# A transformer block with sixteen experts on one core: expert weights in 2 MB blocks with paired rows, and a gathering for two experts at once

## The chip, the core and the metric

The kernel runs on one core of a Trainium2 chip. Five engines work side by side: TensorE (PE, with its weight loads shown apart as PEld), VectorE (DVE), ScalarE (ACT), GpSimd (POOL) and SyncE (SP). Each has its own instruction queue; semaphores order them. In this kernel every transfer between the memory (HBM) and the on-chip buffers is issued by SP and carried by the core's 16 DMA engines. PE reads its operands from the on-chip buffers and writes its sums to the accumulation memory (the tiles `pa`, `pb`, `pd` and `pe`).

The metric is the device time of one execution in microseconds, the median of several runs. MiB below is 1,048,576 bytes; the diff's "2 MB" blocks are 2 MiB.

## The reference, cut to what matters

One layer: normalisation, a joint projection into four kinds of token mixers, an output projection with a gated residual, and then, as the last and longest stage, an expert layer in which every one of 16 experts chooses 64 of the 512 tokens:

```python
def expert_choice_ffn(h, w_router, w_gate, w_up, w_down):
    B, N, D = h.shape
    cap = EC_FACTOR * N // N_EXPERTS
    aff = jax.nn.softmax((h @ w_router).astype(F32), axis=-1)
    gate, idx = lax.top_k(jnp.swapaxes(aff, 1, 2), cap)
    xg = jax.vmap(lambda hb, ib: hb[ib])(h, idx)
    hid = jax.nn.silu(jnp.einsum('becd,edf->becf', xg, w_gate)) * jnp.einsum('becd,edf->becf', xg, w_up)
    y = jnp.einsum('becf,efd->becd', hid, w_down) * gate[..., None].astype(h.dtype)
    return jax.vmap(lambda yb, ib: jnp.zeros((N, D), yb.dtype).at[ib.reshape(-1)].add(yb.reshape(-1, D)))(y, idx)
...
        x_lat = x_lat + m_lat[5] * expert_choice_ffn(h_lat, w_router[l], w_gate[l], w_up[l], w_down[l])
...
    return rmsnorm(x_lat, final_norm_g)
```

Tokens are 1,024 wide, the hidden width of an expert is 2,048, and all is 32-bit floating point. An expert's three weight matrices are 8 MiB each, so an expert reads 24 MiB and the stage 384 MiB, every byte once.

## The kernel before

The program is straight-line code: Python loops unroll into one instruction list for each engine, and a scheduler sets the order on every engine when the program is built. Nearly all compute instructions are recorded in one helper, line 58 (L58), so the trace is read by the names of tiles.

**Routing.** While the output projection still runs, the residual `XL` (four tiles of 128 tokens) is transposed on PE for the router. DVE then finds each expert's 64 tokens in eight rounds of a maximum and a replacement (`RT`); a matmul with a triangular matrix turns the marks into `slot`, which says for each token and expert which of the 64 places it takes. `xn2` holds the normalised tokens, `a2` and `mcol` the scale and shift of each column.

**One expert.** DVE compares `iota` with `slot` to a one-hot matrix `OH` (in tile `OX`). Gathering: 8 matmuls with `OH` as the stationary operand (64 columns) and 512 columns of `xn2` moving, half of the width in each column half of the array; ACT copies the sum to `xgn`, PE transposes it in 8 pieces and DVE applies scale and shift, which gives `xg`, the 64 tokens by columns. Gate and up: 128 rows of a weight matrix at a time (`k` from 0 to 7) are the moving operand, and `xg` is the stationary one; 64 tokens fill half of the array's columns, so two halves of the hidden width are summed in the two column halves (`pgt` and `pup`, both tiles `pb`). ACT and DVE make `hid`, PE transposes it in 8 pieces to `hT`, and 16 row blocks of the down matrix are summed in `pa`. DVE multiplies by the gate of the layer (`m5`) into `y`. `weighted()` multiplies the one-hot matrix by the routing weights `aff` and transposes it (`OT`), and in the next expert four `add` steps multiply `OT` with `y` and add the product into `XL`, one token tile each.

A 32-bit matmul stands in the trace as two records, a transpose as one.

**The weight ring.** `wchunk` takes the next buffer of a ring of 18 of 1 MiB each (128 partitions of 2,048 numbers) and issues one DMA on SP's queue. A gate or up block is 128 weight rows, one row of 8 KB to a partition. A down block is 256 rows; a partition gets two rows of 4 KB that lie apart. The ring's buffers come in three pools, since the space comes free at three times: `ringa` (8) after the mixers, `ringm` (4) during the output projection, `ringb` (6) after it. Expert 0's last gate and up blocks go to four half-size `spare` buffers. Each DMA also waits for the DMA eight places ahead of it on the queue, because eight semaphores are used in turn; so at most eight are under way. SP issues in program order, and a buffer's next DMA waits for the matmuls that read it.

**The end.** The last expert's down product is taken in three blocks of columns (384, 384 and 256), so that the additions, the squares for the final norm (ACT) and the product with `gfin` (POOL) of one block run beside the next one's matmuls; rows of these transfers are 1,536 and 1,024 bytes.

## Time and profile before

| | |
|---|---|
| median of 3 runs | 1511.62 us (1509.63 to 1512.53) |
| the profiled execution's own time | 1509.62 us |
| its span, first to last instruction | 1507.8 us |
| PE busy | 1378.6 us, 91% |
| DVE busy | 458.1 us, 30% |
| ACT busy | 314.1 us, 21% |
| POOL busy | 237.8 us, 16% |
| moved by DMA | 481.57 MB, 319 GB/s over the span |
| granted PE clock, mean | 0.980 |

The page gives busy times, a strip of 40 slices of the span with the granted clock and the DMA rate, the chain of work that ended last, and the costliest groups. The trace behind it answers narrower questions: each engine's timeline, what an engine's queue waited for, busy times and DMA rate in chosen stretches. A busy share is a mean over stages with different limits: the first third of this span has idle DMA engines, the rest has not. The granted clock is a share of full speed: 1.00 is 2.4 GHz, 0.50 is 1.2 GHz.

### The profile page before, as it was taken

Reading aid. Unit: us, or ns where it says so; the run is one execution under the profiler, and the core shown is the slowest. Engines: PE = TensorE matmul, PEld = TensorE weight load, DVE = VectorE, ACT = ScalarE, POOL = GpSimd, SP = SyncE. Lnnn points to the kernel's source line nnn. Section 1 sums busy time; section 2 is a strip of 40 time slices with the busy share of each in tenths; the row PEclk is TensorE's granted clock in tenths of the full one; section 3 lists DMA queues with packets and bytes.
Section 4 is the critical chain, followed back from the end, with each engine's and each line's share of the span. In section 5 each row is a group of like instructions: output and inputs, shape, how many; then the busy total and the mean of one; then the engine's idle time right before and its main releaser. Section 6 shows DMA issues by size and latency. Waiting matters only on the chain.

```text
span 1507.8 us, 20244 instructions
## 1 busy us (share of the span) xinstructions
PE 1378.6 (91%) x8278; PEld 673.1 (45%) x8278; DVE 458.1 (30%) x998; ACT 314.1 (21%) x658; POOL 237.8 (16%) x229
## 2 busy tenths in 40 slices
PE   5998979989889979999999999999999999999996
PEld 3665767767557823333233233332332332333334
DVE  4657732444573640111211211211202112112012
ACT  5424316624573300011010010010010100100103
POOL 2425637431265100000000000000000000000002
PEclk9999989999999979999999999999999999999998
DMA  9341450646883769999999999999999999999995
GB/s 357 116 136 53 119 123 17 178 145 157 259 270 100 323 254 412 414 418 415 414 421 413 416 417 414 418 415 414 420 414 417 418 413 419 415 414 419 414 404 199
DMA packets 128270, 481.57 MB, mean 319 GB/s; under 512 B 34225, under 2 KB 43057, under 8 KB 94514
## 3 DMA queue, kind: packets, MB, share of 16 engines
q1 hardware_dynamic: 128178, 480.29, 82.1%
q8 instruction: 65, 1.06, 0.3%
q14 instruction: 27, 0.22, 0.0%
HBM read 468.84 MB, written 11.40 MB: 318 GB/s over the span
## 4 chain that ended last, share of the span: by engine, by line
PE 75%; DVE 9%; issue 5%; ACT 4%; DMA 3%; POOL 1%; SPq 1%; ACTq 0%; DVEq 0%; POOLq 0%
PE pb L58 33%; PE pa L58 31%; PE pd L58 7%; PE pe L58 5%; DMA wm<-in_wmod 1%; ACT A L58 1%; DVE RT L58 1%; DVE hid L58 1%; DVE tmpb L58 1%; DVE OY L58 1%; ACT hT L58 1%; DMA co<-in_cosq 1%; DVE acc L58 1%; SPq L1054 1%; DVE TB L58 1%
## 5 line engine op out<-in xcount | busy, mean ns | idle before, releaser
L58 PE MATMUL pb<-w,OX 128*64 128x512 f32 x2032 | 453.6, 598 | 0.9 <-DVE OX L58 0.9
L58 PE MATMUL pa<-w,hT 128*64 128x512 f32 (+2 forms) x1152 | 278.9, 549 | 0.1
L58 PEld LDWEIGHTS pb<-w,OX 128*64 128x64 f32 x2032 | 139.9, 137 | 305.2 <-issue 285.9
L1709 POOL TENSOR_TENSOR xo<-XL,gfin 128x384 f32<-128x384 f32 (+1 forms) x12 | 10.6, 913 | 955.9 <-DVE XL L58 955.9
L58 ACT ACTIVATE hid<-pb 128x512 f32<-128x512 f32 x32 | 17.4, 594 | 595.6 <-PE pb L58 595.6
L58 PEld LDWEIGHTS pa<-w,hT 128*64 128x64 f32 x1152 | 89.9, 136 | 114.2 <-issue 108.1
L58 DVE TENSOR_TENSOR hid<-hid,pb 128x512 f32<-128x512 f32 x32 | 20.6, 685 | 276.7 <-PE pb L58 276.7
L58 PE MATMUL pa<-xn,OX 128*64 128x512 f32 x256 | 102.2, 600 | 0.8 <-DVE OX L58 0.8
L58 PE MATMUL pa<-hh,wh 128*128 128x512 f32 (+1 forms) x240 | 89.7, 387 | 7.2 <-DVE dff L58 4.3
L58 PE MATMUL pa<-hh,wl 128*128 128x512 f32 (+1 forms) x240 | 86.2, 372 | 1.3 <-POOL wl L250 1.3
L58 PE MATMUL pd<-OY 64*128 64x512 f32 x120 | 67.3, 641 | 10.3 <-DVE OY L58 10.3
L58 DVE TENSOR_TENSOR XL<-XL,pd 128x512 f32<-128x512 f32 x60 | 41.2, 686 | 100.5 <-PE pe L58 76.5
L58 PE MATMUL pe<-OY 64*128 64x512 f32 x120 | 67.3, 641 | 0.0
L250 POOL TENSOR_TENSOR wl<-wr,wh 128x1024 fp32r<-128x1024 f32 (+1 forms) x22 | 50.7, 2305 | 75.5 <-ACT wh L58 72.9
L58 ACT ACTIVATE xgn<-pa 64x512 f32<-64x512 f32 x32 | 18.9, 592 | 208.7 <-PE pa L58 208.5
L58 DVE TENSOR_TENSOR OX<-OX,aff 128x256 f32<-128x256 f32 x16 | 6.8, 426 | 169.7 <-PE pa L58 169.7
L58 PEld LDWEIGHTS pa<-hh,wh 128*128 128x128 f32 x240 | 47.1, 197 | 23.7 <-issue 5.3
L58 DVE TENSOR_TENSOR XL<-XL,pe 128x512 f32<-128x512 f32 x60 | 41.0, 684 | 50.4 <-PE pd L58 29.0
L58 PE MATMUL pa<-hl,wh 128*128 128x512 f32 (+1 forms) x240 | 55.3, 363 | 0.9 <-POOL hl L334 0.9
L58 PEld LDWEIGHTS pa<-xn,OX 128*64 128x64 f32 x256 | 31.1, 138 | 54.9 <-issue 54.1
L58 PEld LDWEIGHTS pa<-hh,wl 128*128 128x128 f32 x240 | 47.1, 196 | 9.0 <-POOL wl L250 2.3
L58 PEld LDWEIGHTS pa<-hl,wh 128*128 128x128 f32 x240 | 39.7, 188 | 9.0 <-POOL hl L334 1.4
(382 smaller groups left out, 1655.3 us busy)
## 6 DMA issues: line engine op xcount, KB each, us to landing
w<-in_wgate SPq DMA_DIRECT2D x127, 1024.0 KB, 19.9
w<-in_wup SPq DMA_DIRECT2D x127, 1024.0 KB, 19.9
w<-in_wdown SPq DMA_DIRECT2D x122, 1024.0 KB, 18.9
wm<-in_wmod SPq DMA_DIRECT2D x32, 512.0 KB, 7.1
wr<-in_win SPq DMA_DIRECT2D x18, 512.0 KB, 3.4
wm<-in_wmod SPq DMA_DIRECT2D x8, 1024.0 KB, 11.4
w<-in_wdown SPq DMA_DIRECT2D x8, 768.0 KB, 14.5
wr<-in_wout SPq DMA_DIRECT2D x16, 256.0 KB, 6.3
```

What stands on the lines that cost most here:

```text
L58: r = f(*args, **kw)
L250: G.tensor_tensor(wl, raw, wh.bitcast(F32), op=ALU.subtract)
L1054: SY.dma_start(Xh[32 * j:32 * j + 32, c0:c0 + 2 * n].rearrange("d (m t) -> d m t", m=2).bitcast(F32), src[b, x, hs].rearrange("(m d) t -> ...
L1709: G.tensor_tensor(xo[i][:, cols], xl[:, i, cols], gfin[:, cols], op=ALU.mult)
```

## The change

Four things change together, all in the expert stage or for its sake.

1. **Blocks of 2 MiB.** `RW` is 2: a ring buffer holds 4,096 numbers (16 KB) in a partition, and the ring has 5, 2 and 3 buffers, 20 MiB instead of 18. To make room the program's reserve for DMA descriptors is set to 1,024 bytes a partition.
2. **Paired rows.** A gate or up block is 256 weight rows, and a partition gets two neighbouring rows, 16 KB in one piece (`gu_rows`). A down block is 512 rows, four neighbouring rows of 4 KB to a partition, 16 KB in one piece (`d_chunk`, `KD` is 4). The other operand follows: token columns are taken with step 2 (`pair`) in the router's transposes, the layer's scale and shift and the gathering, and the transposes of `hid` take columns with step 4. Some host-side layouts (`bcol`, `g2`, `wr`) are permuted to match. The last expert's column blocks are loaded two transfers to a buffer, with rows of 1,536 and 1,024 bytes as before.
3. **Two experts' gathering.** `pick` makes the one-hot matrix for two experts, and `gather` multiplies `xn2` (stationary, 128 columns with step 2) with it (128 columns moving): 32 matmuls of 128x128 for a pair give `xg` directly; the copy to `xgn` and its transposes are gone, and ACT and DVE apply scale and shift in eight pieces.
4. **Unweighted scatter.** `OT` is the plain one-hot matrix. `y` is split into two parts `yh` and `yl` that are multiplied in the one-pass 32-bit format (F32R), and the routing weight `aff` is applied by DVE when the product is added into `XL`. In the last expert the weight is applied to `y` as a column `share`.

Expert 0 has four `spare` quarter blocks for its last up block only.

The diff, cut to its core ("..." marks what is left out):

```diff
-PA, RA, RM, RB = 2, 8, 4, 6
+PA, RA, RM, RB = 2, 5, 2, 3
+RW, KD = 2, 4
...
+        def pair(k):
+
+            return slice(256 * (k // 2) + k % 2, 256 * (k // 2 + 1), 2)
...
-        def wchunk(src):
+        def wchunk(*srcs):
             n = next(wcount) % (RA + RM + RB)
-            w = tl(rings[0 if n < RA else 1 if n < RA + RM else 2], [128, 2048], "w")
-            SY.dma_start(w if len(src.shape) == 2 else w[:, 0:src.shape[1] * src.shape[2]].rearrange("p (k d) -> p k d", d=src.shape[-1]), src)
+            w = tl(rings[0 if n < RA else 1 if n < RA + RM else 2], [128, RW * 2048], "w")
+            a = 0
+            for src in srcs:
+                n = int(np.prod(src.shape[1:]))
+                v = w[:, a:a + n]
...
+                SY.dma_start(v, src)
             return w
...
+        def gu_rows(ee, c, j):
+
+            return I[("wgate", "wup")[j]][ee, c * 256:(c + 1) * 256, :].rearrange("(p k) f -> p k f", k=2)
+
+        def gu_chunk(ee, c, j):
+
+            src = gu_rows(ee, c, j)
+            if ee == 0 and c == 3 and j in SPARE:
+                if j == SPARE[-1]:
+                    fill_ring()
+                for k in range(2):
+                    for q in range(2):
+                        SY.dma_start(spare[j, k, q], src[:, k, q * 1024:(q + 1) * 1024])
...
         def d_chunk(ee, c):
 
-            return wchunk(I["wdown"][ee, c * 256:(c + 1) * 256, :].rearrange("(k p) d -> p k d", p=128))
+            rows = RW * 256
+            return wchunk(I["wdown"][ee, c * rows:(c + 1) * rows, :].rearrange("(g p k) d -> p g (k d)", p=128, k=KD))
...
-                PE.transpose(pt[:, k * 128:(k + 1) * 128], xl[:, i, k * 128:(k + 1) * 128], ident)
+                PE.transpose(pt[:, k * 128:(k + 1) * 128], xl[:, i, pair(k)], ident)
...
-        spare = [[w4(a, [128, 1024], "spare") for a in ab] for ab in ("BB", "CA")]
+        spare = {(j, k, q): w4("BC"[k], [128, 1024], "spare") for j in SPARE for k in range(2) for q in range(2)}
...
+        def gather(j, h):
...
+                for i in range(4):
+                    PE.matmul(pg[:, k], lhsT=xn2[i][:, pair(k)], rhs=OH2[:, j % 2, i].rearrange("p e c -> p (e c)").bitcast(F32), start=i == 0, stop=i == 3)
...
-            for q in range(2):
-                for i in range(4):
-                    PE.matmul(px[rhalf(q)], lhsT=OH[:, i], rhs=xn2[i][:, q * 512:(q + 1) * 512], start=i == 0, stop=i == 3)
-            for q in range(2):
-                A.activation(xgn[rhalf(q)], px[rhalf(q)], AF.Copy)
-                pt = pa()[:, 0:256].rearrange("p (j c) -> p j c", j=4)
-                for j in range(4):
-                    PE.transpose(pt[:, j], xgn[rhalf(q), j * 128:(j + 1) * 128], ident[rhalf(q), rhalf(q)])
...
-                    PE.transpose(pt[:, j * 128:(j + 1) * 128], hid[:, (4 * n + j) * 128:(4 * n + j + 1) * 128], ident)
+                    g, k = divmod(4 * n + j, KD)
+                    PE.transpose(pt[:, j * 128:(j + 1) * 128], hid[:, 128 * KD * g + k:128 * KD * (g + 1):KD], ident)
...
                 V.tensor_tensor(y, py, m5, op=ALU.mult)
-                def add(i, OT, y):
+                A.activation(yh, y, AF.Copy)
+                V.tensor_tensor(yl, y, yh.bitcast(F32), op=ALU.subtract)
+
+                def add(i, e):
 
                     pc2 = [pde(), pde()]
-                    for h in range(2):
-                        PE.matmul(pc2[h], lhsT=OT[rhalf(h), i * 128:(i + 1) * 128], rhs=y[rhalf(h), :], start=True, stop=True)
+                    for x, yx in enumerate((yh, yl)):
+                        for h in range(2):
+                            PE.matmul(pc2[h], lhsT=OT[rhalf(h), i * 128:(i + 1) * 128], rhs=yx[rhalf(h), :], start=x == 0, stop=x == 1)
                     for h in range(2):
                         xh = halves(xl[:, i])[:, h]
-                        V.tensor_tensor(xh, xh, pc2[h].rearrange("p (b c) -> p b c", c=64), op=ALU.add)
+                        V.scalar_tensor_tensor(xh, pc2[h].rearrange("p (b c) -> p b c", c=64), aff[:, i, e:e + 1], xh, op0=ALU.mult, op1=ALU.add)
...
-            for n, (c0, c1, kbs) in enumerate(((0, 384, (4,) * 4), (384, 768, (4,) * 4), (768, 1024, (8, 8)))):
+            for n, (c0, c1, kbs) in enumerate(((0, 384, (8, 8)), (384, 768, (8, 8)), (768, 1024, (8, 8)))):
...
-                V.tensor_tensor(y[:, yc], py[:, 0:hw], m5[:, yc], op=ALU.mult)
+                V.scalar_tensor_tensor(y[:, yc], py[:, 0:hw], share, m5[:, yc], op0=ALU.mult, op1=ALU.mult)
...
-    nc = _bacc.Bacc("TRN2", target_bir_lowering=False, num_devices=1)
+    nc = _bacc.Bacc("TRN2", target_bir_lowering=False, num_devices=1, dynamic_dma_scratch_size=1024)
```

What it does to the order on the engines, at three places. The first is SP's queue while the ring is first filled (`w` are ring buffers, `spare` the extra ones); before, from the 13th ring buffer on:

```order
L1426 DMA w_5408<-in_wgate 128x2048
L1426 DMA w_5410<-in_wup 128x2048
L1436 DMA spare_5302<-in_wgate 128x1024
L1436 DMA spare_5303<-in_wgate 128x1024
L1426 DMA w_5423<-in_wdown 128x2x1024
L1426 DMA w_5425<-in_wdown 128x2x1024
L1426 DMA w_5427<-in_wdown 128x2x1024
L1426 DMA w_5429<-in_wdown 128x2x1024
L1436 DMA spare_5304<-in_wup 128x1024
L1436 DMA spare_5305<-in_wup 128x1024
L1426 DMA w_5487<-in_wdown 128x2x1024
L1426 DMA w_5493<-in_wdown 128x2x1024
```

and now, from the 5th on:

```order
L1438 DMA w_5392<-in_wgate 128x4096
L1438 DMA w_5394<-in_wup 128x4096
L1438 DMA w_5412<-in_wgate 128x4096
L1438 DMA w_5414<-in_wdown 128x4096
L1438 DMA w_5416<-in_wdown 128x4096
L1438 DMA w_5418<-in_wdown 128x4096
L1453 DMA spare_5304<-in_wup 128x1024
L1453 DMA spare_5305<-in_wup 128x1024
L1453 DMA spare_5306<-in_wup 128x1024
L1453 DMA spare_5307<-in_wup 128x1024
L1438 DMA w_5495<-in_wdown 128x4096
L1438 DMA w_5510<-in_wgate 128x4096
```

Up to the first buffer that is used a second time (`w_5487` before, `w_5495` now) SP issues 18 MiB of ring and 2 MiB of spare before, 20 and 2 now; three of expert 0's four down blocks are among them, where it was four of eight.

The second place is PE between two experts; `pa` is the down product (`w` with `hT`), `OX` or `OH` the one-hot matrix. Before, the next expert's gathering and its transposes stand among the down product's matmuls:

```order
L58 MATMUL pa_5974<-xn_838_5245,OX_5972 64x512
L58 MATMUL pa_5974<-xn_839_5246,OX_5972 64x512
L58 MATMUL pa_5974<-xn_840_5247,OX_5972 64x512
L58 MATMUL pa_5922<-w_5947,hT_965_5897 64x512 x4
L58 MATMUL pa_5985<-ident_83,xgn_5975 128x64 x4
L58 MATMUL pa_5993<-ident_83,xgn_5975 128x64
L58 MATMUL pa_5922<-w_5953,hT_965_5897 64x512 x4
L58 MATMUL pa_5993<-ident_83,xgn_5975 128x64 x3
L58 MATMUL pa_5922<-w_5959,hT_965_5897 64x512 x4
L58 MATMUL pa_5922<-w_5965,hT_965_5897 64x512 x4
L58 MATMUL pd_6014<-OY_5920 128x512
```

Now it stands so after every second expert:

```order
L59 MATMUL pb_5637<-OH_5302,xn_837_5244 128x128
L59 MATMUL pb_5637<-OH_5302,xn_838_5245 128x128
L59 MATMUL pb_5637<-OH_5302,xn_839_5246 128x128
L59 MATMUL pb_5637<-OH_5302,xn_840_5247 128x128
L59 MATMUL pa_5690<-w_5691,hT_867_5441 64x512 x5
L59 MATMUL pa_5690<-w_5701,hT_867_5441 64x512 x8
L59 MATMUL pa_5690<-w_5711,hT_867_5441 64x512 x8
L59 MATMUL pa_5690<-w_5721,hT_867_5441 64x512 x8
L59 MATMUL pb_5734<-w_5736,xg_5303 64x512 x8
L59 MATMUL pd_5748<-yhl_5442,OT_5443 128x512
L59 MATMUL pe_5749<-yhl_5442,OT_5443 128x512
```

The gathering is in matmuls of 128x128 with nothing after them on PE, the additions (`pd` and `pe` from `yhl`) follow the down product at once or after the next expert's first block, and eight matmuls read one buffer where it was four.

The third place is the end on PE: `pa` is the last expert's down product in its column blocks (`64x192` and `64x128`), `pb` the scatter of the block before. Before:

```order
L58 MATMUL pa_8927<-w_8958,hT_1568_8907 64x192 x8
L58 MATMUL pb_8970<-OY_8864 128x192 x2
L58 MATMUL pb_8976<-OY_8864 128x192 x2
L58 MATMUL pa_8994<-w_8995,hT_1568_8907 64x192
L58 MATMUL pb_8982<-OY_8864 128x192 x2
L58 MATMUL pb_8988<-OY_8864 128x192 x2
L58 MATMUL pa_8994<-w_8995,hT_1568_8907 64x192 x7
L58 MATMUL pa_8994<-w_9005,hT_1568_8907 64x192 x8
L58 MATMUL pa_8994<-w_9015,hT_1568_8907 64x192 x8
L58 MATMUL pa_8994<-w_9025,hT_1568_8907 64x192 x8
L58 MATMUL pb_9037<-OY_8864 128x192 x2
L58 MATMUL pb_9043<-OY_8864 128x192 x2
```

and now:

```order
L59 MATMUL pa_8538<-w_8558,hT_867_5441 64x192 x16
L59 MATMUL pb_8584<-hid_5440,OT_5443 128x192 x2
L59 MATMUL pb_8590<-hid_5440,OT_5443 128x192 x2
L59 MATMUL pa_8608<-w_8609,hT_867_5441 64x192
L59 MATMUL pb_8596<-hid_5440,OT_5443 128x192 x2
L59 MATMUL pb_8602<-hid_5440,OT_5443 128x192 x2
L59 MATMUL pa_8608<-w_8609,hT_867_5441 64x192 x15
L59 MATMUL pa_8608<-w_8628,hT_867_5441 64x192 x16
L59 MATMUL pa_8672<-w_8673,hT_867_5441 64x128 x3
L59 MATMUL pb_8648<-hid_5440,OT_5443 128x192 x2
L59 MATMUL pb_8654<-hid_5440,OT_5443 128x192 x2
L59 MATMUL pa_8672<-w_8673,hT_867_5441 64x128 x2
```

There are two waits for a buffer in a column block where there were four, and the second half of the second block's scatter stands behind five matmuls of the third block instead of behind one.

## Rows read from the trace of the kernel before

**Rows 1.** Stretches: start:end, length, each engine's busy time, PEclk, DMA share, GB/s.

```profile
520.00:530.00 10.00, 8.67 (x82) 7.89 (x81) 6.58 (x29) 3.43 (x12) 3.37 (x3) 1.00 0.19 48
550.00:560.00 10.00, 8.24 (x30) 2.93 (x30) 1.94 (x5) 2.47 (x3) 0.00 (x0) 0.84 0.01 4
1300.00:1400.00 100.00, 95.11 (x424) 31.58 (x424) 17.85 (x31) 5.19 (x9) 0.00 (x0) 1.00 1.02 417
1462.00:1482.00 20.00, 18.53 (x134) 9.61 (x130) 2.61 (x5) 4.08 (x7) 0.18 (x1) 1.00 1.04 361
1487.00:1488.00 1.00, 1.00 (x12) 0.62 (x8) 0.00 (x0) 0.00 (x0) 0.00 (x0) 1.00 0.06 20
```

**Rows 2.** The chain that ended last, pieces on PE: start, us, what.

```profile
645.73 20.03 PE pa L58 x96
...
701.98 15.28 PE pa L58 x76
...
1115.45 15.28 PE pa L58 x76
...
1174.52 15.28 PE pa L58 x76
```

**Rows 3.** What SP's queue waited for, 600 to 700 us: total us, times, longest.

```profile
SPq L1426 <- PE pb L58: 57.6, 29, 10.5
```

**Rows 4.** The same, 1300 to 1400 us.

```profile
SPq L1426 <- DMA w<-in_wgate: 29.2, 14, 2.1
...
SPq L1426 <- PE pb L58: 13.3, 7, 4.4
```

**Rows 5.** SP's queue in order of time, 1022 to 1107 us: start, duration, what.

```profile
1022.37 22.73 SPq L1426 DMA_DIRECT2D w<-in_wdown  x8
1045.19 2.31 SPq L1426 DMA_DIRECT2D w<-in_wgate  x1
...
1050.89 0.33 SPq L1426 DMA_DIRECT2D w<-in_wup  x1
...
1058.58 0.33 SPq L1426 DMA_DIRECT2D w<-in_wgate  x1
...
1071.54 0.33 SPq L1426 DMA_DIRECT2D w<-in_wup  x1
...
1081.51 0.33 SPq L1426 DMA_DIRECT2D w<-in_wup  x1
...
1106.01 2.31 SPq L1426 DMA_DIRECT2D w<-in_wgate  x1
```

**Rows 6.** The page's DMA issues: count, KB each, median us from issue to landing.

```profile
w<-in_wgate SPq DMA_DIRECT2D x127, 1024.0 KB, 19.9
```

**Rows 7.** SP's queue when expert 0 begins, columns as in rows 5.

```profile
560.83 5.81 SPq L1426 DMA_DIRECT2D w<-in_wdown  x4
```

**Rows 8.** PE's timeline: start, us, operation, count, idle time before and its releaser.

```profile
504.87 0.60 PE L58 MATMUL pb<-ident,XL 128*128 128x128 f32 x4
...
541.14 1.13 PE L58 MATMUL pb<-xn,ident 128*128 128x512 f32 x2
...
557.44 25.95 PE L58 MATMUL pb<-w,OX 128*64 128x512 f32 x112 [0.92 <-DVE OX L58]
...
1454.86 17.39 PE L58 MATMUL pb<-w,OX 128*64 128x512 f32 x80
...
1490.74 3.71 PE L58 MATMUL pa<-w,hT 128*64 128x128 f32 x62
```

**Rows 9.** Groups of one expert by form, 645.73 to 701.98 us: busy us, mean ns.

```profile
L58 PE MATMUL pb<-w,OX 128*64 128x512 f32 x128 | 28.1, 594 | 0.0
...
L58 PE MATMUL pa<-xn,OX 128*64 128x512 f32 x16 | 5.4, 595 | 0.0
...
L58 PE MATMUL pa<-ident,xgn 64*128 64x64 f32 x8 | 0.8, 221 | 0.0
```

More of the change, by code (lines that the diff above doesn't have):

```diff
@@ new lines, in pick @@
+        def pick(j):
+            shp = [128, 4, 2, CAP]
+            V.tensor_tensor(OH2[:, j % 2], bc(iota.unsqueeze(1).unsqueeze(1), shp), bc(slot[:, :, 2 * j:2 * j + 2].unsqueeze(3), shp), op=ALU.is_equal)
+        pgs = {}
+        def gather(j, h):
+            if not h:
+                pgs[0] = pb().rearrange("p (k c) -> p k c", k=8)
+            pg = pgs[0]
+            for k in range(4 * h, 4 * h + 4):
+                for i in range(4):
+                    PE.matmul(pg[:, k], lhsT=xn2[i][:, pair(k)], rhs=OH2[:, j % 2, i].rearrange("p e c -> p (e c)").bitcast(F32), start=i == 0, stop=i == 3)
+            for k in range(4 * h, 4 * h + 4):
+                o = xg[:, k].rearrange("p e c -> p (e c)")
+                if k % 2:
+                    A.activation(o, pg[:, k], AF.Identity, bias=mcol[:, 24 + k, 0:1], scale=a2[:, k:k + 1])
+                else:
+                    V.tensor_scalar(o, pg[:, k], a2[:, k:k + 1], mcol[:, 24 + k, 0:1], op0=ALU.mult, op1=ALU.add)
@@ new lines, in build, with sums @@
+        pick(0)
+        for h in range(2):
+            gather(0, h)
+        for ee in range(last + 1):
+            pgt, pup = pb(), pb()
+            def sums(p, w, c, order):
+                for k, n in order:
+                    for q in range(2):
+                        PE.matmul(p[rhalf(q), n * 512:(n + 1) * 512], lhsT=xg[:, 2 * c + k, ee % 2], rhs=w(k, q, n),
+                                  start=c == 0 and k == 0, stop=c == 3 and k == 1)
+            for c in range(4):
+                if ee < last and ee % 2 == 1 and c == 1:
+                    pick(ee // 2 + 1)
+                wg_, wu_ = (gu_chunk(ee, c, j) for j in range(2))
+                by_n = [(k, n) for n in range(2) for k in range(2)]
+                by_k = [(k, n) for k in range(2) for n in range(2)]
+                sums(pgt, wg_, c, by_k)
+                if adds:
@@ L1638, in build @@
                 V.tensor_tensor(hid[:, ns], hid[:, ns], pup[:, ns], op=ALU.mult)
-            hT2 = w4("C", [128, 1024], "hT2")
+            po = pde()
+            for i in range(4):
+                for q in range(2):
+                    PE.matmul(po[rhalf(q), i * 128:(i + 1) * 128], lhsT=OH2[:, ee // 2 % 2, i, ee % 2].bitcast(F32), rhs=ident, start=True, stop=True)
+            A.activation(OT, po, AF.Copy)
+            more = ee < last and ee % 2 == 1
+            if more:
+                gather(ee // 2 + 1, 0)
             hv2 = hT2.rearrange("p (j q c) -> p j q c", q=2, c=CAP)
@@ L1672, in build @@
             r3 = {}
-            small = w4("B", [128, 3, 4], "small")
+            pga, small, share = pde(), w4("C", [128, 3, 4], "small"), tl(sm, [128, 1], "share")
+            for q in range(2):
+                for i in range(4):
+                    PE.matmul(pga[rhalf(q), 0:1], lhsT=OH2[:, ee // 2 % 2, i, ee % 2].bitcast(F32), rhs=aff[:, i, ee:ee + 1], start=i == 0, stop=i == 3)
+            V.tensor_copy(share, pga[:, 0:1])
+            gfin = w4("A", [128, D], "gfin")
+            SY.dma_start(gfin[0:1], I["gfin"].unsqueeze(0))
             A.activation(small[:, 0, 0:1], iota[:, 0:1], AF.Sqrt)
@@ L1699, in build @@
                         f += 1
-                V.tensor_tensor(y[:, yc], py[:, 0:hw], m5[:, yc], op=ALU.mult)
-                junk = w4("C", [128, 512], "fj")
+                V.scalar_tensor_tensor(y[:, yc], py[:, 0:hw], share, m5[:, yc], op0=ALU.mult, op1=ALU.mult)
+                if not n:
+                    for m in range(2):
+                        pg = pde()
+                        PE.matmul(pg, lhsT=selb[0:1, :], rhs=gfin[0:1, m * 512:(m + 1) * 512], start=True, stop=True)
+                        A.activation(gfin[:, m * 512:(m + 1) * 512], pg, AF.Copy)
+                junk = hid[:, 512:1024]
                 for i in range(4):
```

98 lines of the change are left out of this document (38 added, 60 removed).

## The prediction, made before the changed kernel ran

> **What bounds the kernel now.** PE is busy for 91% of the span, which says little, so I read the stretches first [rows 1]. There the reader sees the DMA engines idle before the expert stage (share 0.19 from 520 to 530 us, 0.01 from 550 to 560), at a share of 1.02 and 417 GB/s inside it, and idle again from 1487 (0.06). The first ring buffer that is used a second time is issued at 560.83 [rows 7], so the DMA engines work without a break for some 926 us, until about 1487.2.
>
> Then the chain that ended last [rows 2]. In it the stage is PE, without a DMA: from one expert's down product to the next it takes 56.25 us early (645.73 to 701.98) and 59.07 later (1115.45 to 1174.52).
>
> How both can be full is told by the waits of SP's queue. Early SP waits for matmuls to release a buffer, 57.6 us of 100 [rows 3]; late it waits for a transfer eight places ahead, 29.2 us on gate blocks alone, and for matmuls only 13.3 [rows 4]. PE begins with 20 MiB in hand. The DMA engines bring an expert in 60.82 us (1045.19 to 1106.01) [rows 5], PE eats one in 56 to 59, and what it has in hand shrinks until the end. So the two limits lie within 3% of each other. A faster PE alone would run into the DMA engines; the time can fall by more only if the transfers get shorter too.
>
> **Longer rows in a partition.** SP's issues wait for the block eight places ahead, so their spacing is the time of one landed block. Gate and up blocks, 128 rows of 8 KB to the MiB: four spacings from 1071.54 to 1081.51, 2.49 us each. Down blocks, 256 rows of 4 KB: three from 1050.89 to 1058.58, 2.56 us [rows 5]. So 128 more rows cost 0.07 us, and if the price is per row, 64 rows of 16 KB save half of that, 0.035, and a MiB takes 2.46. The short rows of the last expert bear the form out: 361 GB/s [rows 1] is 2.90 us per MiB, and the same line gives 2.42 + 0.07 x 683/128 = 2.79 for rows of 1,536 bytes. Gate and up of experts 1 to 15 are 240 MiB x 0.035 = 8.4 us; the down blocks still to come, 14 x 8 + 2 = 114 MiB, go from 2.56 to 2.46, 0.105 x 114 = 12.0. Sum 20.4 us, all of it on the DMA engines' unbroken work. Bounds: 16 KB rows are no better than 8 KB rows (only the down blocks gain, 0.07 x 114 = 8.0), or the row price vanishes (0.07 x 240 + 0.14 x 114 = 32.8). A loss is a rival below.
>
> Blocks of 2 MiB as such I cost at nothing: a gate block lands 19.9 us after its issue [rows 6], which is eight blocks of 2.49, so its fixed part is hidden behind seven others. The Trainium skill (DMA: Bandwidth & Descriptors, section Anatomy of one DMA) gives a DMA from GpSimd some 2.0 us of fixed time beside its bytes at 436 GB/s. By that alone a MiB would take 4.4 us in blocks of 1 MiB and 3.4 in blocks of 2, and the change would save hundreds of microseconds; the spacing of 2.49 shows that it does not add up here.
>
> **Two MiB more before the start.** 22 MiB instead of 20 are issued before expert 0 releases a buffer. The DMA engines are idle from 550 to 560 [rows 1], so the extra blocks cost nothing there and are missing later: 2 x 2.56 = 5.1 us. The other two thirds of the filling wait for the same releases as before.
>
> **The start.** Before, gate matmuls start at 557.44 [rows 8] and the next DMA is issued at 560.83 [rows 7]. Now the gathering's first half is 16 matmuls, 32 records of 128x128, then scale and shift, then the gate block, with the second half of the gathering among its first matmuls; and a buffer is released after 16 records instead of 8. No row shows such a record with a stationary operand taken in steps. Nearest are the transposes of 128x128, four in 0.60 us; far off is the 128x512 record, two in 1.13 [rows 8], a quarter of which is 0.14. I take 0.15, a little more in the first half, since the clock there is low (0.84 in the mean [rows 1]). The first half ends about 553.5, scale and shift 0.8 us later, and the buffer comes free after 16 gate records (3.5 us) and the second half (32 x 0.15 = 4.8), at 562.7: 1.9 us later. Bounds: 1 us earlier to 8 later, if steps double the loads in the router's transposes too. After that PE releases 2 MiB every 3.5 us (16 records of 0.216: 17.39 us for 80 [rows 8]), faster than the 4.9 that they take to load.
>
> **PE in an expert.** 56.25 us early [rows 2], of which the gathering and its transposes are 5.4 + 0.8 [rows 9]. Now half of a pair's gathering, 32 records, and about 1.3 us until `yh` and `yl` stand where `y` stood before. At 0.11 to 0.32 a record (transposes in a row; 0.14 plus a load that nothing covers) that gives 54.8 to 61.6; at 0.13, close to the transposes, 55.5. The DMA engines need 24 x 2.46 plus the 0.44 us by which today's expert exceeds 16 x 2.49 + 8 x 2.56, 59.4. Below 57 us PE's period is covered: it uses up its 22 MiB and then waits for blocks. What it saves is worth nothing but the end.
>
> **The end.** Before, the last matmuls of the last column block end at 1490.74 + 3.71 = 1494.45 [rows 8], 7.2 us after the last landing, and 13.4 us of additions, norm and output follow. Now PE waits for the last buffer and needs half of those records, 1.9 us, and some 0.5 for what stands before them: 15.8 us after the landing instead of 20.6. If PE is as far behind as now, nothing is gained here.
>
> **Sum.** Last landing 1487.2 - 20.4 - 5.1 + 1.9 = 1463.6; span 1479.4; with the 1.8 us that the profiled execution has outside its span (1509.62 to 1507.8), 1481.2 against its 1509.62. The runs' median lies 2.0 above that execution; I add half: **1482**.
>
> **Rivals.**
> - *Rows of 16 KB bring nothing over 8 KB*, or the transfers are cut into shorter pieces, so that the change does not do what it says. For: only two lengths of long rows are in the trace. The sum loses 12.4 us: 1494. Chance 0.18.
> - *PE stays the bound, slower.* Place: the 32 gathering records of an expert and the transposes of `hid`, with operands in steps of 2 and 4 that no row shows. At 0.32 us a record an expert takes 61.6, and 557.4 + 27.9 (expert 0's gate and up) + 15 x 61.6 + 35.6 (from 1472.25, the end of the last gate and up [rows 8], to the end of the span) is 1545. It decides from a period of 57 us and is slower than before from 59.2. Against: the contiguous transposes load as many columns in 0.15 us or less. Chance 0.05.
> - *Rows of 16 KB are slower than 8 KB ones*, say at today's 2.56 us: gate and up lose 0.07 x 240 = 16.8, down gains nothing: 1482 + 37 = 1519. It is slower than before from 2.54 us per MiB. No row points that way. Chance 0.06.
> - *The clock falls while PE waits for blocks.* After the short waits before 557.44 the granted clock fell, and the first 8 gate records took 3.4 us (to 560.83) instead of 1.7 [rows 7, 8]. While PE is behind it does not wait, so this can cost only near the end, up to some 12 us of its matmuls: 1494. Chance 0.04. The Trainium skill (TensorE: Matmul & The Clock Gate, section HAM oscillation) tells of a kernel whose matmuls waited for a DMA at every tile and ran at the low clock each time; here the stage shows 1.00 throughout so far.
> - *The row price vanishes and the start is early:* 1468. Chance 0.07.
>
> **How the numbers follow.** My forecast has the remaining 0.60, about 1474 to 1489 by itself. The range of 1470 to 1497 takes in the first rival and the clock and leaves out most of the best case and the two slow ones. About 0.2% is what a measurement of this kernel can tell from no change. Faster: 0.60 + 0.18 + 0.04 + 0.07 less what the tails of these cases lose, 0.86; slower 0.11; the same 0.03.
>
> **What would show it.** Right: the DMA engines at a share near 1.0 from about 563 to 1464; gate issues of 2 MiB spaced 4.9 us; an expert's period near 59 us in the second half with PE waiting on `w`; GB/s up from 417 to about 424; a granted clock of 1.00. Wrong: spacing of 5.0 or more (rows bring nothing), a period without waits on `w` (PE bound), or a break in the DMA strip, which would mean that a released buffer comes too late for blocks of 2 MiB.

## The result and the profile after

The changed kernel takes 1485.31 us in the median of four runs (1484.53 to 1490.35) against 1511.76 before: a ratio of 0.9835, with a 95% interval of 0.9814 to 0.9856. The forecast was 1482, with a range of 1470 to 1497. The profiled execution has 1486.06 us and a span of 1484.2, where the prediction had 1481.2 and 1479.4. The sign and the main mechanism were right. One term of the sum, the end, was too small by 5.9 us, and the others gave a little back.

The page of the changed kernel, its busy line of TensorE and the strip of 40 slices (a slice is 37.1 us):

```profile
PE 1329.8 (90%) x8422; PEld 708.6 (48%) x8422; DVE 452.4 (30%) x958; ACT 321.9 (22%) x675; POOL 237.9 (16%) x229
...
PEclk9999989999999989999999999999999999999998
DMA  9341450456684867999999999999999999999995
GB/s 355 118 144 55 107 139 17 144 178 167 231 239 157 340 283 327 427 425 428 426 427 427 427 425 428 426 427 427 427 427 425 429 425 427 427 427 426 427 402 188
```

PE has 49 us less work than before and the span is only 24 shorter, so the span does not follow PE's work alone. The GB/s strip shows the transfers' part: about 427 in every slice of the expert stage until the last two, where it was 417 [rows 1].

Stretches of the changed kernel, columns as in [rows 1] (length, busy time of PE, PEld, DVE, ACT, POOL, granted clock, DMA share, GB/s):

```profile
550.00:560.00 10.00, 10.00 (x69) 8.46 (x68) 0.82 (x2) 0.92 (x2) 0.00 (x0) 0.85 0.02 9
560.00:570.00 10.00, 10.00 (x52) 3.93 (x52) 0.82 (x2) 2.20 (x3) 0.00 (x0) 1.00 0.54 190
1300.00:1400.00 100.00, 92.68 (x478) 37.24 (x472) 12.64 (x20) 8.01 (x15) 0.00 (x0) 1.00 1.01 427
1440.00:1460.00 20.00, 18.48 (x138) 11.48 (x140) 3.74 (x7) 5.70 (x14) 3.09 (x4) 0.91 1.01 341
...
1462.00:1462.50 0.50, 0.50 (x11) 0.45 (x8) 0.00 (x0) 0.00 (x0) 0.00 (x0) 1.00 0.31 102
1462.50:1463.00 0.50, 0.50 (x11) 0.48 (x8) 0.00 (x0) 0.00 (x0) 0.00 (x0) 1.00 0.22 57
```

The DMA engines are idle from 550 to 560, as before, then at a share of 1.01, and the last weights land about 1462.5. I call that the last landing: the end of the last half microsecond with over 100 GB/s. Before, by the same measure, it is 1487.0. Here are SP's issues when expert 0 begins and late, and what its queue waited for from 1300 to 1400 us (total, times, longest), which answer [rows 7, 5 and 4]:

```profile
563.82 0.33 SPq L1438 DMA_DIRECT2D w<-in_wdown  x1
567.28 0.33 SPq L1438 DMA_DIRECT2D w<-in_wgate  x1
...
1382.12 0.33 SPq L1438 DMA_DIRECT2D w<-in_wup  x1
...
1401.73 0.33 SPq L1438 DMA_DIRECT2D w<-in_wup  x1
```

```profile
SPq L1438 <- DMA w<-in_wup: 29.5, 7, 4.5
SPq L1438 <- DMA w<-in_wdown: 29.2, 7, 4.5
SPq L1438 <- DMA w<-in_wgate: 24.5, 6, 4.5
SPq L1438 <- PE pa L59: 3.8, 2, 2.8
SPq L1438 <- PE pb L59: 3.8, 3, 2.1
```

Four spacings from 1382.12 to 1401.73 are 4.90 us each, 2.45 us per MiB; the prediction had 2.46. SP waits for transfers 83.2 us of 100. Two numbers now stand for the whole stage. The **stretch** is the time from the first reused buffer's issue to the last landing: 1462.5 - 563.82 = 898.7 us for 362 MiB, against 1487.0 - 560.83 = 926.2 us for 364 MiB before. The rest, from the last landing to the end of the span, is 21.7 us (before 20.8; the prediction read its last landing as 1487.2).

### The profile page after: what moved, and what is told of

Same layout as the page of the kernel before. It is cut to its first block, busy times and chain, and to the rows that moved or that the text cites. A ratio compares the mean times of both kernels' runs of the same rounds, so it can differ in the third digit from the quotient of the medians.

```text
span 1484.2 us, 20090 instructions
## 1 busy us (share of the span) xinstructions
PE 1329.8 (90%) x8422; PEld 708.6 (48%) x8422; DVE 452.4 (30%) x958; ACT 321.9 (22%) x675; POOL 237.9 (16%) x229
## 4 chain that ended last, share of the span: by engine, by line
PE 61%; DMA 13%; DVE 9%; ACT 4%; issue 3%; POOL 1%; SPq 1%; ACTq 0%; DVEq 0%; POOLq 0%
PE pb L59 33%; PE pa L59 19%; DMA w<-in_wdown 8%; PE pd L59 5%; PE pe L59 5%; DMA w<-in_wup 3%; DMA wm<-in_wmod 2%; ACT A L59 1%; DVE XL L59 1%; DVE RT L59 1%; DVE hid L59 1%; DVE tmpb L59 1%; DVE yhl L59 1%; ACT hid L59 1%; ACT yhl L59 1%
## 5 line engine op out<-in xcount | busy, mean ns | idle before, releaser
L59 PE MATMUL pb<-w,xg 128*64 128x512 f32 x2032 | 458.3, 601 | 2.2 <-DMA w<-in_wup 1.3
L59 PEld LDWEIGHTS pb<-w,xg 128*64 128x64 f32 x2032 | 147.5, 138 | 274.9 <-issue 263.0
L59 PE MATMUL pa<-w,hT 128*64 128x512 f32 (+2 forms) x1152 | 234.4, 550 | 7.6 <-DMA w<-in_wdown 5.6
L59 PEld LDWEIGHTS pb<-OH,xn 128*128 128x128 f32 x512 | 63.5, 200 | 25.1 <-ACT hid L59 12.4
L59 PE MATMUL pb<-OH,xn 128*128 128x128 f32 x512 | 67.7, 290 | 8.2 <-ACT hid L59 7.1
L59 DVE TENSOR_TENSOR hid<-pa,XL 128x512 f32<-128x512 f32 x15 | 10.4, 692 | 208.0 <-PE pa L59 208.0
L59 DVE SCALAR_TENSOR_TENSOR XL<-pe,aff,XL 128x512 f32<-128x512 f32 x60 | 44.8, 747 | 76.2 <-PE pd L59 70.2
L59 PE MATMUL pe<-yhl,OT 64*128 64x512 f32 x120 | 47.4, 458 | 17.7 <-ACT yhl L59 10.2
L59 PE MATMUL pd<-yhl,OT 64*128 64x512 f32 x120 | 47.4, 458 | 15.9 <-ACT yhl L59 8.7
L59 DVE SCALAR_TENSOR_TENSOR XL<-pd,aff,XL 128x512 f32<-128x512 f32 x60 | 44.8, 746 | 50.4 <-PE pe L59 46.4
```

Source lines behind the costliest of these rows:

```text
L59: r = f(*args, **kw)
```

## The experiments

All stretches in one table. "First reuse" is SP's issue of the first ring buffer that is used a second time; times in us, medians of the whole runs.

| kernel | median | first reuse | last landing | stretch | MiB in it |
|---|---|---|---|---|---|
| before | 1511.76 | 560.83 | 1487.0 | 926.2 | 364 |
| changed | 1485.31 | 563.82 | 1462.5 | 898.7 | 362 |
| e1, rows of 8 and 4 KB in 2 MiB blocks | 1509.45 | 566.62 | 1487.0 | 920.4 | 362 |
| e2, rows of 8 KB in 2 MiB blocks | 1502.64 | 566.46 | 1479.0 | 912.5 | 362 |
| e3, blocks of 1 MiB, rows of 8 KB | 1500.57 | 561.98 | 1475.5 | 913.5 | 362 |
| e4, ring of 18 MiB | 1491.45 | 564.71 | 1468.0 | 903.3 | 364 |
| e5, changed, less work on PE | 1485.24 | 563.71 | 1462.0 | 898.3 | 362 |
| e6, before, less work on PE | 1507.12 | 561.30 | 1487.0 | 925.7 | 364 |
| e7, before, down rows of 8 KB | 1511.46 | 560.17 | 1478.5 | 918.3 | 364 |
| e8, gathering in quarters | 1482.95 | 555.56 | 1459.5 | 903.9 | 362 |
| e9, `gfin` spread by its transfer | 1481.77 | 560.61 | 1460.5 | 899.9 | 362.5 |
| e10, square root's table later | 1483.99 | 567.38 | 1466.0 | 898.6 | 362 |
| e11, e8 to e10 together | 1481.61 | 556.02 | 1461.5 | 905.5 | 362.5 |
| e12, changed again | 1483.81 | 561.26 | 1460.0 | 898.7 | 362 |

The theory: the stage is set by the transfers from the first reuse on, and rows of 16 KB and two MiB more in hand shortened it. The rivals: larger blocks as such brought the rate; TensorE was the limit and its own saving was paid out.

**e1 and e2: is it the rows or the blocks?** Both keep blocks of 2 MiB and change only which rows a partition gets.

```diff
 # e1
-            return I[("wgate", "wup")[j]][ee, c * 256:(c + 1) * 256, :].rearrange("(p k) f -> p k f", k=2)
+            return I[("wgate", "wup")[j]][ee, c * 256:(c + 1) * 256, :].rearrange("(k p) f -> p k f", k=2)
...
-            return wchunk(I["wdown"][ee, c * rows:(c + 1) * rows, :].rearrange("(g p k) d -> p g (k d)", p=128, k=KD))
+            return wchunk(I["wdown"][ee, c * rows:(c + 1) * rows, :].rearrange("(k p) d -> p k d", p=128))
 # e2: the first as in e1, and
+            return wchunk(I["wdown"][ee, c * rows:(c + 1) * rows, :].rearrange("(g p k) d -> p g (k d)", p=128, k=2))
```

> The changed kernel with its blocks of 2 MiB, its ring and its instruction order kept, but with the rows of before inside a block: a gate or up block brings a partition two weight rows of 8 KB that lie apart, a down block four of 4 KB that lie apart (so the weights meet other columns of the operands than they should; the work and the bytes are the same). Row theory (the price is per row, the blocks' size is worth nothing): gate issues spaced 2 x 2.49 = 4.98 us and down issues 5.12 us where the changed kernel has 4.90; 240 MiB x 0.038 + 114 MiB x 0.107 = 21.3 us longer, about 1506.6 us. Rival (larger blocks bring the rate, rows do not matter): spacing stays 4.90 and the time 1485.

> As the run before, but every row is 8 KB: gate and up blocks bring two rows of 8 KB that lie apart, down blocks two pieces of 8 KB that lie apart (again the weights meet other columns). Row theory: spacing 4.98 us for all blocks, 354 MiB x 0.037 = 13.1 us longer than the changed kernel, 1498.4 us; between this and the run before 114 MiB x 0.07 = 8.0 us. If only the 4 KB rows cost and 8 KB rows are as good as 16 KB rows: 1485 to 1487. If rows do not matter: 1485.

Measured: 1509.45 and 1502.64. Their stretches are 21.7 and 13.8 us longer than the changed kernel's, for 21.3 and 13.1 expected; the medians lie 3 to 4 us above the expectation and the first reuse came 2.7 us later in both: the gathering began 1.4 to 1.6 us later than in the changed kernel and its first half took 1.2 us longer (the last section tells of such shifts). So the rows carry the gain: 13.8 us over 354 MiB is 0.039 us per MiB from 8 KB to 16 KB, and 920.4 - 912.5 = 7.9 us over 114 MiB is 0.069 from 4 KB to 8 KB. The prediction had 0.035 and 0.07. The same stretch, 1300 to 1400 us, of e1 and of e2:

```profile
1300.00:1400.00 100.00, 88.38 (x442) 35.08 (x444) 16.98 (x26) 6.34 (x12) 0.00 (x0) 0.98 1.02 418
```

```profile
1300.00:1400.00 100.00, 91.37 (x458) 36.34 (x456) 16.98 (x26) 7.42 (x14) 0.00 (x0) 0.98 1.01 420
```

With the rows of before, blocks of 2 MiB give 418 GB/s, where the kernel before gave 417 with blocks of 1 MiB.

**e3: the blocks alone.** The changed kernel with 20 buffers of 1 MiB and rows of 8 KB.

```diff
-PA, RA, RM, RB = 2, 5, 2, 3
-RW, KD = 2, 4
+PA, RA, RM, RB = 2, 10, 4, 6
+RW, KD = 1, 2
...
-            for n, (c0, c1, kbs) in enumerate(((0, 384, (8, 8)), (384, 768, (8, 8)), (768, 1024, (8, 8)))):
+            for n, (c0, c1, kbs) in enumerate(((0, 384, (4,) * 4), (384, 768, (4,) * 4), (768, 1024, (8, 8)))):
```

> The changed kernel with blocks of 1 MiB in a ring of 20 (same 20 MiB ring, same two MiB of spare, same bytes ahead); rows of 8 KB everywhere (one row of a pair to a gate or up block, two neighbouring rows to a down block). Row theory: as with rows of 8 KB in blocks of 2 MiB, 13 us longer than the changed kernel, less up to 1.7 us because the first buffer comes free after 8 records instead of 16: 1497 to 1499. Theory that a DMA has a fixed cost that blocks of 2 MiB halve: clearly longer than the run with 2 MiB blocks and 8 KB rows, by 0.3 us or more for each of some 180 further DMAs, 1550 or more.

Measured: 1500.57. The stretch is 913.5, 1.0 us longer than e2's with the same rows and twice the DMAs. Divided by the 177 ring DMAs that blocks of 1 MiB need more, that is 6 ns each. Blocks of 2 MiB as such are worth 1 us at most. The Trainium skill (DMA: Bandwidth & Descriptors, section Anatomy of one DMA) gives some 2.0 us of fixed time to a DMA from GpSimd; on SP's queue with eight under way nothing of that size comes out between e2 and e3.

**e4: two MiB more in hand.** One ring buffer fewer.

```diff
-PA, RA, RM, RB = 2, 5, 2, 3
+PA, RA, RM, RB = 2, 5, 2, 2
```

> The changed kernel with nine ring buffers of 2 MiB instead of ten, 18 MiB as before, 2 MiB less in hand when the experts begin. If the transfers are the limit from the first reused buffer to the end: the 2 MiB are moved later at 2.45 us per MiB, 4.9 us longer, 1490.2 us. If TensorE is the limit with transfers hidden: no change, 1485. If the ring's depth is what keeps TensorE from waiting between experts: more than 10 us longer, with breaks in the DMA strip.

Measured: 1491.45, 6.1 us longer; the stretch is 4.6 us longer, for 4.9 expected, and the first reuse was 0.9 later. The DMA strip has no breaks. The ring's size is worth the time of what it moves ahead and nothing else.

**e5 and e6: TensorE's work taken away.** Only one of an expert's four additions remains, in the changed kernel (e5) and in the kernel before (e6).

```diff
 # e5
-                adds = [(add, i, ee) for i in range(4)]
+                adds = [(add, i, ee) for i in range(1)]
 # e6
-                adds = [(add, i, OT, y) for i in range(4)]
+                adds = [(add, i, OT, y) for i in range(1)]
```

> The changed kernel with only one of an expert's four additions (the scatter into token tile 0; the tiles 1 to 3 get no expert's output but the last one's), so each expert has some 5 us less of TensorE's work. If the transfers are the limit: the last weight still lands near 1462.5 us, TensorE waits for blocks from the first experts on, and the time moves by less than 2 us, 1483 to 1486. If TensorE is the limit: 15 x 5 = 75 us shorter, 1410.

> The kernel before with only one of an expert's four additions (as in the run before this one): some 6.8 us less of TensorE's work in an expert, its transfers unchanged. Theory that both limits stand side by side and the transfers come right behind TensorE: the last weight lands at 1487 us as before, TensorE is no longer behind, the last gate and up product ends with its block's landing at about 1467 instead of 1472.25, and the time falls by about 5 us to 1506. If TensorE alone is the limit before: 15 x 6.8 = 100 us shorter, 1410. If transfers alone: no change, 1511.

Measured: 1485.24, no change, and 1507.12, 4.6 us less than before (a ratio of 0.9972, 0.9962 to 0.9981). That is the transfers' answer both times. What PE waited for, in e5 from 560 to 1450 us and in e6 from 560 to 1470 (total, times, longest):

```profile
PE pb L59 <- DMA w<-in_wup: 20.7, 20, 1.3
PE pa L59 <- DMA w<-in_wdown: 18.8, 17, 2.6
PE pb L59 <- DMA w<-in_wgate: 18.8, 18, 1.3
```

```profile
PE pb L58 <- DMA w<-in_wup: 17.3, 32, 0.6
PE pb L58 <- DMA w<-in_wgate: 16.4, 29, 0.7
```

The time that PE was given it spent waiting for weights, 58 us in e5 (7.8 in the changed kernel) and 34 in e6; in the kernel before it has no such wait in the whole stage. The expectations took off too much, 75 and 100 us: PE's busy time from 560 to 1460 us fell by 28 us in e5, with 23 us of waits for `XL` gone besides, and by 34 in e6. So the times forecast there for TensorE as the limit were too low as well; that PE waited for weights in both rules it out all the same. In e6 the last landing stayed at 1487.0, and only the lag at the end went: the last gate and up block was waited for and its eight records ran from 1465.32 to 1467.26, where the kernel before ended that product at 1472.25 [rows 8].

**e7: shorter transfers alone.** The kernel before with its down rows in pairs, 8 KB in one piece.

```diff
-            return wchunk(I["wdown"][ee, c * 256:(c + 1) * 256, :].rearrange("(k p) d -> p k d", p=128))
+            return wchunk(I["wdown"][ee, c * 256:(c + 1) * 256, :].rearrange("(p k) d -> p k d", p=128))
```

> The kernel before with longer rows in its down blocks alone: a partition gets two neighbouring rows, 8 KB in one piece, instead of two that lie apart (so the weights meet other columns of the hidden layer than they should). The transfers get 116 MiB x 0.07 = 8.1 us shorter. Theory that both limits stand side by side: TensorE's matmuls, which wait for no block before, take as long as ever, and the time stays at 1511 within 2 us, while the last weight lands some 8 us earlier. If the transfers alone are the limit before: 1503.

Measured: 1511.46, no change, with the stretch 7.9 us shorter (8.1 expected). So the kernel before stood at both limits: less work on PE brought 4.6 us, shorter transfers alone nothing. Only a change of both could bring 26. Which of the changed kernel's edits to PE's work made the room, the gathering for two or the new scatter, no run separates.

**e8: the idle time before the first reuse.** The first pair's gathering in quarters of 8 matmuls, the first ahead of expert 0's gate block.

```diff
-        def gather(j, h):
+        def gather(j, k0, k1):
...
-            for k in range(4 * h, 4 * h + 4):
+            for k in range(k0, k1):
...
-        for h in range(2):
-            gather(0, h)
+        gather(0, 0, 2)
...
                 sums(pup, wu_, c, by_n if c == 3 else by_k)
+                if not ee and c < 3:
+                    gather(0, 2 * c + 2, 2 * c + 4)
```

> The changed kernel with the first pair's gathering in four quarters instead of two halves, the first quarter ahead of expert 0's first gate block and the others between its blocks, so that the first ring buffer comes free sooner. If the idle time of the DMA engines between the filled ring and the first reuse (550 to 564 us) is paid in full at the end: the first reuse is issued at about 557 instead of 563.8, and the time falls by 4 to 7 us, less what the next buffers come late by (each still stands behind a quarter), to about 1480. If the end is set by TensorE from the last up block alone, independent of that start: no change, 1485.

Measured: 1482.95, 2.4 us less than the changed kernel and 0.9 less than the same kernel in e12, less than expected either way. SP's issues in e8 as expert 0 begins:

```profile
555.56 0.33 SPq L1438 DMA_DIRECT2D w<-in_wdown  x1
561.87 0.33 SPq L1438 DMA_DIRECT2D w<-in_wgate  x1
568.18 0.33 SPq L1438 DMA_DIRECT2D w<-in_wup  x1
575.35 0.33 SPq L1438 DMA_DIRECT2D w<-in_wgate  x1
```

The first comes 8.3 us earlier, but the next ones 6.3 to 7.2 us apart, behind the other quarters, where a block needs 4.9. The DMA engines wait between them, the stretch is 5.2 us longer, and 3 of the 8 us arrive at the last landing. Part of that is the execution: PE began the gathering at 547.82 here and at 549.03 in the changed kernel. Counted from there the first reuse comes some 7 us earlier and the last landing 1.8.

**e9, e10, e11 and e12: the end.** The missed term was 5.9 us after the last landing. Here is PE at the end of the changed kernel (start, us, operation, count, wait before it):

```profile
1436.04 3.65 PE L59 MATMUL pb<-w,xg 128*64 128x512 f32 x16 [0.89 <-DMA w<-in_wgate]
1441.00 3.65 PE L59 MATMUL pb<-w,xg 128*64 128x512 f32 x16 [1.30 <-DMA w<-in_wup]
1444.58 1.12 PE L59 MATMUL pe<-gfin,selb 1*128 1x512 f32 x2
...
1446.31 1.17 PE L59 MATMUL pd<-gfin,selb 1*128 1x512 f32 x2
...
1448.47 6.48 PE L59 MATMUL pa<-w,hT 128*64 128x192 f32 x64
...
1465.89 3.27 PE L59 MATMUL pa<-w,hT 128*64 128x128 f32 x54
```

PE waits for a weight for the last time at 1441.00, the last up block, which landed at 1440.95. From there it needs 28.2 us to its last down matmul (1469.17), while the last down weights land after 21.6. So PE does not stand waiting for the last down block, as the prediction took for granted, but is behind it. And ACT, on the way to the output:

```profile
1472.85 1.28 ACT L59 ACT_TABLE_LOAD   x1
```

The kernel before loads that table for the square root ahead of its last two column blocks; in the changed kernel the early square root that should bring it was moved up by the scheduler, before expert 15's `silu`, whose own table then took its place. The factor `gfin` lies in one row, and two products with `selb` spread it to all partitions; in e9 the transfer does that. Three edits test these two pieces:

```diff
 # e9
-            SY.dma_start(gfin[0:1], I["gfin"].unsqueeze(0))
+            SY.dma_start(gfin, I["gfin"].partition_broadcast(128))
...
-                if not n:
-                    for m in range(2):
-                        pg = pde()
-                        PE.matmul(pg, lhsT=selb[0:1, :], rhs=gfin[0:1, m * 512:(m + 1) * 512], start=True, stop=True)
-                        A.activation(gfin[:, m * 512:(m + 1) * 512], pg, AF.Copy)
 # e10
-            A.activation(small[:, 0, 0:1], iota[:, 0:1], AF.Sqrt)
...
+                    if n == 0 and i == 3:
+                        A.activation(small[:, 0, 0:1], s3[:, i, n:n + 1], AF.Sqrt)
 # e11: e8, e9 and e10 together; e12: the changed kernel
```

> The changed kernel whose final norm's factor gfin is brought to all 128 partitions by the transfer itself (0.5 MiB) instead of one row and two products with selb on TensorE and two copies on ACT, which stand between the last up block and the last down product. Theory on the missed term (after the last up block lands at 1440.95 the end is one chain on TensorE of 28.2 us to the last down matmul, while the transfers still to come need 21.8 us): the chain loses two products of 1.1 us less the 0.9 us that the transposes would wait for hid anyway, about 1.4 us, and the transfers' extra 1.2 us cost nothing; some 1484. Theory of the prediction (TensorE waits for the last down block and the end follows its landing): 1.2 us longer, 1486.5.

> The changed kernel with the one early square root that brings ACT's table placed behind the first column block's squares, so that no other function's table is loaded between it and the end. In the changed kernel ACT loads a table at 1472.85 for 1.28 us, inside the chain that ends last, where the kernel before had it loaded at 1475.01, ahead of its last two column blocks. If that load is part of the missed term: 1.3 us shorter, 1484, and no table load within the last 15 us. If the chain there is hidden behind the other square roots and the output: no change.

> The changed kernel with three edits: the first pair's gathering in quarters (measured alone: 2.4 us), gfin spread by its transfer, the square root's table loaded behind the first squares. If the three lie on one path: 2.4 + 1.4 + 1.3 = 5 us shorter than the changed kernel, 1480. If the earlier start and the shorter chain at the end hide one another: 1482 to 1483.

> The changed kernel once more, on the chip of the three runs before it, so that differences of one to five microseconds are taken on one chip: 1485.3 within 2 us.

Measured: 1481.77, 1483.99, 1481.61 and 1483.81. Between executions the first reuse moves by several microseconds, so these medians don't settle differences of one or two; the traces do. From the landing of the last up block to the last down matmul e12 takes 26.7 us (1438.22 to 1464.94) and e9 25.8 (1437.30 to 1463.10): 0.9 less, with 0.5 MiB more to transfer, for 1.4 expected. So the chain on PE sets that part, and not the transfers. From the last down matmul to the end of the span e12 takes 15.1 us and e10 14.0 (1470.88 to 1484.9), as the first output leaves 2.1 us after the last square instead of 3.2: 1.1 of the 1.3 us expected. e11 with the same edit has 14.0 too (1465.52 to 1479.5), e9 without it 15.0. In e10 the table is loaded here:

```profile
1461.08 1.28 ACT L59 ACT_TABLE_LOAD   x1
```

Together they don't add up. In e11 PE, with less in its way, waits for down weights again:

```profile
1451.81 0.51 PE L59 MATMUL pa<-w,hT 128*64 128x192 f32 x2 [0.52 <-DMA w<-in_wdown]
...
1457.93 2.14 PE L59 MATMUL pa<-w,hT 128*64 128x192 f32 x22 [0.56 <-DMA w<-in_wdown]
```

e9 and e11 lie 2.0 and 2.2 us below e12 on the same chip. Against the kernel before their ratios are 0.9804 (0.9785 to 0.9822) and 0.9805 (0.9788 to 0.9821), e12's is 0.9815 (0.9799 to 0.9831): the intervals overlap, and I don't call either faster than the changed kernel.

## Why the prediction was right, and where it was not

| step | predicted | measured |
|---|---|---|
| longer rows | 20.4 us less | 21.7 less (e1) |
| blocks of 2 MiB as such | 0 | 1.0 less (e3 against e2) |
| 2 MiB more in hand | 5.1 less | 4.6 less (e4) |
| first reuse | 562.7 | 563.8; 561.3 in e12 |
| last landing | 1463.6 | 1462.5; 1460.0 in e12 |
| PE's time for an expert, before it waits | 55.5 | 56.9 to 57.7 |
| last landing to the end of the span | 15.8 | 21.7; 20.0 in e12 |

**Two limits side by side: right.** e6 and e7 moved one limit each and found the other at once.

**The rows: right, mechanism and size.** The form taken from two lengths of rows in [rows 5], a price per row that halves when the row doubles, holds at 16 KB. For short rows it holds less well: the prediction's own 2.90 us against 2.79 is 4% off, where the step from 8 to 16 KB is worth 1.4%, so those rows bore nothing out; e1 and e2 do. The rivals in which 16 KB rows bring nothing or cost something fall with e1 and e2.

**Two MiB in hand, and the blocks: right.** e4 and e3 give 4.6 and 1.0 us, and the stretch of e1, which has both but not the rows, is 5.8 shorter than before.

**The start: right, within an execution's chance.** The gathering's first half ended at 554.6 (552.0 in e12) for 553.5. A gathering record of 128x128 was put at 0.15 us in the first half; it took 0.17 (5.57 us for 32) at a granted clock of 0.85 and 0.13 (4.04 for 32) at 1.00. The rival with records of 0.32 us falls.

**PE's time for an expert: too small by 1.4 to 2.2 us, without effect.** The records came out as taken, the waits did not. This is PE behind a down product of the changed kernel:

```profile
824.02 0.49 PE L59 MATMUL pe<-yhl,OT 64*128 64x512 f32 x1 [1.46 <-ACT yhl L59]
...
824.75 0.50 PE L59 MATMUL pe<-yhl,OT 64*128 64x512 f32 x1 [0.23 <-DVE yhl L59]
...
825.18 5.35 PE L59 MATMUL pb<-w,xg 128*64 128x512 f32 x16
...
832.04 0.73 PE L59 MATMUL pe<-yhl,OT 64*128 64x512 f32 x2 [0.84 <-DVE XL L59]
...
838.51 1.09 PE L59 MATMUL pe<-ident,OH 128*64 128x128 f32 x16 [0.84 <-DVE XL L59]
...
857.96 2.15 PE L59 MATMUL pb<-OH,xn 128*128 128x128 f32 x16 [1.19 <-ACT hid L59]
```

The wait for `yh` and `yl` was predicted (1.3 us, it is 1.46 + 0.23); the two of 0.84 us for DVE, which now multiplies by `aff` as it adds, were not, nor the 16 records at 5.35 us instead of 3.65 (the granted clock from 825 to 830 is 0.66). From 742.49 to 857.96 two experts take 115.5 us, and the next two, without records at the low clock, 113.8 (to 971.73). That is right at the 57 us that the prediction named as the bound of its cover: PE's first wait for a block ended at 1164.80, and it waited for 7.8 us in all. e5 shows that less work brings nothing more. More work would soon have cost: 7.8 us over 15 experts is an estimated 0.5 us an expert, and beyond that PE would have come last to the last up block. So the two limits still stand side by side.

**The end: the step that was mis-sized.** The prediction let PE wait for the last down block and do half a column block's records after it, 2.4 us, and then 13.4 us as before. Measured: 6.7 and 15.0. The first part misses that PE, even when it is ahead in the experts, comes to the down product behind: it waits for the last up block, and from there its own work (the rest of the product, two products for `gfin`, the transposes, the column blocks and the additions between them) is 6.6 us longer than the transfers still to come. The prediction had named this case (if PE is as far behind as now, nothing is gained here) but gave it no place in the sum; the rest after the last landing was 20.8 us before and is 21.7 now. Of the 6.6 us 1.4 are the clock: four transposes took 1.13 us here and 0.75 in e12, the first column block's 64 records 6.48 and 5.42. The second part misses the table load; what the diff shows is a line that did not change, and only the order on ACT tells that it came to stand elsewhere. Last landing 1.1 early and end 5.9 late: 1479.4 became 1484.2. The forecast of the median is only 3.3 us low because the profiled execution lies 0.8 above the median here, where before it lay 2 below; that is chance.

**The clock as a rival: a small part of it.** The granted clock fell four times in the stage and once at the end, where PE had waited for two blocks; the mean from 1446 to 1451 is 0.66. It cost 1.4 us there, not 12, and the profiled execution of e12, with the same two waits, has 1.00 from 1440 to 1460. The first two falls came before PE had waited for any block: the means from 825 to 830 and from 1055 to 1060 are 0.66 and 0.69, right behind the waits for `yh` and `yl`, 1.46 and 0.23 us both times. In e5, where PE waited for blocks 55 times, 8 of the 17 means of 50 us from 600 to 1450 lie below 1.00 (the lowest 0.93), where in the changed kernel it is 5 and in e12 3 (the lowest 0.97 in both). The Trainium skill (TensorE: Matmul & The Clock Gate, section HAM oscillation) tells of a kernel whose matmuls waited for a DMA at every tile, longer than here, and ran at the low clock each time; here more waits go with more falls, but most waits are followed by none. What decides it these runs leave open.

## What to carry to other kernels

Where a transfer's issue waits for the transfers ahead of it, read its price from the spacing of issues, split it by the length of the rows, and forecast the time of the whole unbroken stretch from its first to its last byte: the differences worked out so came out within 1 us here (e1, e2, e4, e7), and the prediction's own stretch, 1463.6 - 562.7 = 900.9, was 2.2 us too long. The block size changed it by 1 us and the work of the engine beside it by half of one. When two limits stand side by side, moving one brings next to nothing, and one run for each shows it. Then work the end out as a stage of its own: follow the last consumer back to the last block it will really wait for, add all its work from there, and look on every engine for instructions that the scheduler has moved, a table load among them.

## What the runs showed that was not expected

**A fall of the clock 100 us ahead of the first reuse shifts the whole run.** e12, the changed kernel and e10 run the same program up to the end. Here are, in this order, the stretch from 450 to 460 us, where PE has waited for a weight of the stage before (`wm`), and the first half of the gathering:

```profile
450.00:460.00 10.00, 7.82 (x57) 5.57 (x57) 4.75 (x9) 6.92 (x16) 8.57 (x8) 1.00 0.88 326
546.70 5.33 PE L59 MATMUL pb<-OH,xn 128*128 128x128 f32 x32 [1.04 <-DVE OH L59]
```

```profile
450.00:460.00 10.00, 7.08 (x40) 5.06 (x41) 4.15 (x9) 4.93 (x12) 6.58 (x6) 0.83 0.91 333
549.03 5.57 PE L59 MATMUL pb<-OH,xn 128*128 128x128 f32 x32 [1.04 <-DVE OH L59]
```

```profile
450.00:460.00 10.00, 6.71 (x32) 4.71 (x34) 3.72 (x7) 5.02 (x11) 7.00 (x6) 0.76 0.95 350
551.36 6.79 PE L59 MATMUL pb<-OH,xn 128*128 128x128 f32 x32 [1.04 <-DVE OH L59]
```

At 411 us the three are within 0.4 us of each other on PE. By 464 the changed kernel is 2.4 us behind e12 and e10 4.7, in the order of the clocks 1.00, 0.83 and 0.76, and by as much the gathering begins later. Its first half then takes 5.33, 5.57 and 6.79 us, as the clock from 550 to 560 is 1.00, 0.85 and 0.66. The first reuse came at 561.26, 563.82 and 567.38, and the stretch behind it was 898.7, 898.7 and 898.6. So these microseconds go through to the end one for one, and an experiment of 2 us on this kernel is read from the stretch, not from the median. When the clock falls there stays open: a wait for `wm` of 3.02 us in e3 was followed by 1.00, one of 2.76 in e1 by 0.55.

**An issue can hold SP longer.** With blocks of 256 rows of 8 KB (e2), two issues late in the stage keep SP 4.6 us each, and not 0.33:

```profile
1329.13 4.58 SPq L1438 DMA_DIRECT2D w<-in_wgate  x1
1333.80 4.58 SPq L1438 DMA_DIRECT2D w<-in_wup  x1
```

The DMA engines' share stayed at 1.01, so it cost nothing here. It is not a matter of the issue's own rows alone: in e2 the issue at 566.46 took 0.38 us and the one behind these two 0.42, and in the kernel before a gate block of 128 rows took 2.31 us behind eight down blocks and a block of as many rows 0.33 further on [rows 5]. That SP is held by what is still queued would fit, but no run tests it.
